# Attention on one core: the first pair's queries transposed in two copies at once, and the second pair's query load on another queue

## The chip, the cores and the metric

The kernel runs on one core of one Trainium2 chip. The metric is the device time of one execution in microseconds (us). Before the change the median of five runs is 123.73 us, the lowest 123.12 and the highest 124.13.

## The reference

Plain softmax attention over 8 batches of 8 heads, 512 positions and 64 features per head, float32 in and out:

```
scores = einsum('bhqd,bhkd->bhqk', q, k) / sqrt(64)
attn   = softmax(scores, axis=-1)
out    = einsum('bhqk,bhkd->bhqd', attn, v)
```

## The kernel before

**Tiling.** The 64 heads are taken in 32 pairs. A pair's q, k and v (256 KB each) are loaded whole, as tiles of 128 partitions by 2 heads by 4 rows by 64 features: every partition holds 4 successive rows of each head. They are cast to float16, q and k are transposed on TensorE (PE) so that the 64 features lie on partitions, and the transposes are copied out of PSUM by VectorE (DVE) (line 353 for pair 1, which is the second pair; line 355 for the later ones). A block of scores is one head's 128 keys by 512 queries (line 374). Two blocks make a group, and one exponential of ScalarE (ACT, line 379) of 128 by 1024 turns a group into float16 weights. There are 129 groups; six of them are raised on DVE instead (lines 393 to 435). The weights are multiplied with v and a column of ones (line 462), DVE divides (lines 440 and 441), and the result is stored.

**Order.** The order of PE and DVE work after the opening is written by a planner from fixed costs (class `Plan`), while the kernel is built; the order of the instructions on every engine is therefore fixed, and none of it depends on what the chip does. The exponentials run in one order on ACT. PE's score tiles are three deep.

**Loads.** Loads are issued by SyncE's queue (SP), in a fixed order: k and q, then v, pair after pair, some pairs ahead. The first loads stand in `first_loads` (lines 501 to 508): the first pair's keys in two halves on ACT's queue and its queries in two halves on SP's queue; then the second pair's keys on SP (line 507) and the second pair's queries on ACT (line 508). Eight completion counters are used in turn by all loads, so a ninth load is issued only when the first has landed, and so on.

**The opening** (`first_pair`, lines 514 to 598). The first pair is cast by three engines: DVE takes queries 0 and 1 of head 0 (line 522) and keys 0 and 1 (line 523), ACT takes queries 2 and 3 (line 524) and the whole of head 1's keys (line 526), GpSimd (POOL) takes keys 2 and 3 (line 525) and the whole of head 1's queries (line 527). The scores of the first pair need the queries on both halves of the partitions, since the keys of two chunks lie one above the other. Before, one cast copy of the queries is transposed twice, once into partitions 0 to 63 and once into partitions 64 to 127 (`t_q`, lines 545 to 547). The keys need one transpose for two chunks (`t_k`, line 541). DVE copies queries, keys, queries, keys (lines 573 to 576) and the scores follow (line 552), with the exponentials of line 559. `busy` (line 512) are matmuls on constants that keep PE running.

**The second pair.** POOL casts its keys, DVE its queries (line 331); PE transposes first the keys, then the queries (line 348); DVE copies both halves (line 353) after the last of the eight transposes; the scores of line 374 follow.

Of the kernel before, what the change touches and what calls it, by code (L numbers as in the profile page):

```python
# [9 lines left out]
FP16 = mybir.dt.float16  # L10
# [219 lines left out]
def kernel(  # L230
# [7 lines left out]
    nc = tc.nc  # L238
    B, H, S, D = q.shape
    P = 128  # L240
    NI = S // P
# [20 lines left out]
    cpool = ctx.enter_context(tc.tile_pool(name="const", bufs=1))  # L262
# [16 lines left out]
    ident = cpool.tile([P, P], FP16, name="ident")  # L279
# [13 lines left out]
    def source(src, g):  # L293
        b, h = g // ppb, 2 * (g % ppb)
        return src[b, h : h + 2].rearrange("h (p i) d -> p h i d", i=NI)

    def load_tile(g, name):
        t = lpool.tile(
            [P, 2, NI, D],
            FP32,  # L300
            tag=f"{name}32",
            name=f"{name}32_{g}",
            bufs=6,
        )
        raw.setdefault(g, {})[name] = t
        return t

    def load(g, names):
        if g >= NP:
            return  # L310
        for name in names:
            src = {"q": q, "k": k, "v": v}[name]
            t = load_tile(g, name)
            if name == "v" and g in HALVED:
                for h in range(2):
                    nc.sync.dma_start(out=t[:, h], in_=source(src, g)[:, h])
                continue
            nc.sync.dma_start(out=t[:, :, :, :], in_=source(src, g))

    def cast_v(g):  # L320
        if g >= NP:
            return
        nc.gpsimd.tensor_copy(out=vps[g % NV][:, :, :, 0:D], in_=raw[g]["v"][:, :, :, :])  # L323

    def cast_qk(g):
        if g >= NP:
            return
        t = qpool.tile([P, 2, NI, P], FP16, tag="qkp", name=f"qkp_{g}")
        for n, name in ((1, "k"), (0, "q")):
            eng = nc.vector if (g, name) == (1, "q") else nc.gpsimd  # L330
            eng.tensor_copy(  # L331
                out=t[:, n].rearrange("p i (h d) -> p h i d", h=2),
                in_=raw[g][name][:, :, :, :],
            )
        qkp[g] = t

    def feed(g):
        load(g + 5, "kqv")
        cast_qk(g + 3)
        cast_v(g + 2)  # L340
# [9 lines left out]
    def copy(g):  # L350
        if g == 1:
            for n in (1, 0):
                nc.vector.tensor_copy(out=tqk[g][:, n], in_=tps[g][:, n].rearrange("p i c -> p (i c)"))  # L353
            return
        nc.vector.tensor_copy(  # L355
            out=tqk[g][:, :, :], in_=tps.pop(g).rearrange("p n i c -> p n (i c)")
        )
# [143 lines left out]
    def first_loads():  # L501
        tk = load_tile(0, "k")
        tq = load_tile(0, "q")
        for h in range(2):
            nc.scalar.dma_start(out=tk[:, h], in_=source(k, 0)[:, h])
            nc.sync.dma_start(out=tq[:, h], in_=source(q, 0)[:, h])  # L506
        nc.sync.dma_start(out=load_tile(1, "k"), in_=source(k, 1))
        nc.scalar.dma_start(out=load_tile(1, "q"), in_=source(q, 1))

    def busy(dst, n):  # L510

        nc.tensor.matmul(dst[:, 0:n], ones[:, 0:P], ones[:, 0:n], start=True, stop=True)  # L512

    def first_pair():

        tk, tq = raw[0]["k"], raw[0]["q"]
        k16 = cpool.tile([P, 2, NI, D], FP16, name="k16_0")
        q16 = cpool.tile([P, 2, NI, D], FP16, name="q16_0")
        kt = cpool.tile([P, 2, 2, P], FP16, name="kt_0")
        qt = cpool.tile([P, 2, NI, P], FP16, name="qt_0")  # L520

        nc.vector.tensor_copy(out=q16[:, 0, 0:2], in_=tq[:, 0, 0:2])
        nc.vector.tensor_copy(out=k16[:, 0, 0:2], in_=tk[:, 0, 0:2])
        nc.scalar.copy(q16[:, 0, 2:4], tq[:, 0, 2:4])  # L524
        nc.gpsimd.tensor_copy(out=k16[:, 0, 2:4], in_=tk[:, 0, 2:4])
        nc.scalar.copy(k16[:, 1], tk[:, 1])
        nc.gpsimd.tensor_copy(out=q16[:, 1], in_=tq[:, 1])

        st0, pka, st1 = (
            ps_st.tile([P, 2, S], FP32, tag="st", name=f"st_{n}") for n in ("0a", "ka", "1")  # L530
        )
        pqa = ps_x.tile([P, 8, P], FP16, tag="x0", name="tp_qa")
        pqb = ps_x.tile([P, 8, P], FP16, tag="x1", name="tp_qb")

        pka, pkc, pqc = pka[:, 0, :], st1[:, 0, :], st1[:, 1, :]
        pka, pkc, pqc = (
            t.bitcast(FP16).rearrange("p (n c) -> p n c", c=P) for t in (pka, pkc, pqc)
        )

        def t_k(dst, h, j):  # L540
            nc.tensor.transpose(
                dst, k16[:, h, 2 * j : 2 * j + 2, :].rearrange("p i d -> p (i d)"), ident
            )

        def t_q(dst, h, i):
            for x in range(2):
                nc.tensor.transpose(dst[64 * x : 64 * x + 64], q16[:, h, i, :], ident)

        def first_scores(st, h, j, q0, q1, pt, s0, s1):
            for x in range(2):  # L550
                s = slice(64 * x, 64 * x + 64)
                nc.tensor.matmul(
                    st[:, x, s0:s1],
                    kt[s, h, j, :],
                    qt[s, h].rearrange("p i c -> p (i c)")[:, q0:q1],
                    start=True,
                    stop=True,
                )
            nc.scalar.activation(
                out=pt[:, :, q0:q1], in_=st[:, :, s0:s1], func=EXP, scale=scale  # L560
            )

        for n in range(6):
            busy(st0[:, 0], S)
        for n in range(2):
            busy(st0[:, 0], P)
        for i in range(2):
            t_q(pqa[:, i], 0, i)
        for i in range(2):
            t_q(pqc[:, i], 0, 2 + i)  # L570
        t_k(pka[:, 0], 0, 0)
        t_k(pkc[:, 0], 0, 1)
        nc.vector.tensor_copy(out=qt[:, 0, 0:2], in_=pqa[:, 0:2])
        nc.vector.tensor_copy(out=kt[:, 0, 0], in_=pka[:, 0])
        nc.vector.tensor_copy(out=qt[:, 0, 2:4], in_=pqc[:, 0:2])
        nc.vector.tensor_copy(out=kt[:, 0, 1], in_=pkc[:, 0])
        for n in range(3):
            busy(st0[:, 1], P)
        pts = [ppool.tile([P, 2, S], FP16, tag="pt", name=f"pt_{m}") for m in range(3)]
        for m in range(3):  # L580
            for x, b in enumerate(groups[m]):
                blocks[b] = pts[m][:, x, :]
        first_scores(st0, 0, 0, 0, 256, pts[0], 0, 256)
        st0b = ps_st.tile([P, 2, S], FP32, tag="st", name="st_0b")
        first_scores(st0b, 0, 0, 256, 512, pts[0], 0, 256)
        first_scores(st1, 0, 1, 0, S, pts[1], 0, S)
        for i in range(NI):
            t_q(pqb[:, i], 1, i)
        nc.vector.tensor_copy(out=qt[:, 1], in_=pqb[:, 0:4])
        pkb = ps_x.tile([P, 8, P], FP16, tag="x0", name="tp_kb")  # L590
        for j in range(2):
            t_k(pkb[:, j], 1, j)
        nc.vector.tensor_copy(out=kt[:, 1], in_=pkb[:, 0:2])
        st2 = ps_st.tile([P, 2, S], FP32, tag="st", name="st_2")
        for n in range(4):
            busy(st2[:, 0], P)
        first_scores(st2, 1, 0, 0, S, pts[2], 0, S)
        first.update(kt=kt, qt=qt)

    with tc.manual_schedule():  # L600
        first_loads()
        load(0, "v")
        for g in range(2, 5):
            load(g, "kq")
            load(g - 1, "v")
        load(4, "v")
        make_identity(nc, ident)
        for n in range(NV):
            nc.vector.memset(vps[n][:, :, :, D : D + 1], 1.0)
        first_pair()  # L610
        cast_qk(1)
        cast_v(0)
        cast_qk(2)
        cast_v(1)
        feed(0)
        do = {
            "transposes": transposes,
            "scores": scores,
            "values": values,
            "feed": feed,  # L620
            "raise": raise_,
            "copy": lambda g, b: copy(g),
            "pass": pass_,
            "norm": lambda u, n, b: normalise(u, n),
        }
        for what, *args in Plan(groups, NP, 3).run():
            do[what](*args)
# [30 lines left out]
```

## Time and profile before

| | |
|---|---|
| median of five runs | 123.73 us (123.12 to 124.13) |
| the profiled execution's own time | 124.2 us |
| its span, first to last instruction | 122.4 us |
| mean granted TensorE clock | 0.995 |
| ACT busy | 114.2 us (93% of the span) |
| PE busy | 107.7 us (88%) |
| DVE busy | 99.6 us (81%) |
| POOL busy | 74.5 us (61%) |
| DMA | 33.82 MB, 276 GB/s in the mean |

The profile is one execution, and the times of its rows are counted from the start of the span, so 1.8 us of that execution's own time lie around the span. PE is matmul, PEld is its weight load, SP and ACTq are the queues that issue loads. A busy share is the mean over stages with different limits. Matmul rows show a modelled end: what can be read from them is when one starts after another.

### The profile page before, as it was taken

The numbers are of one execution on the slowest core, as the hardware profiler recorded it, in microseconds if no ns is written. First come the engines' busy times: TensorE is split into PE (matmuls) and PEld (weight loads), VectorE is DVE, ScalarE is ACT, GpSimd is POOL, SyncE is SP. The second block draws the span as 40 slices with busy tenths as digits, with TensorE's granted clock in tenths as the row PEclk, the third lists the DMA queues.
The fourth block names the chain that finished last, engine by engine and source line by source line (L and its number), as shares of the span: only waits on it lengthen the run. The fifth ranks groups of instructions, "written<-read, shape, count | busy, mean of one in ns | idle before, by whom it ended". The sixth has DMA issues, their size and how long they took to land.

```text
span 122.4 us, 3967 instructions
## 1 busy us (share of the span) xinstructions
PE 107.7 (88%) x1565; PEld 67.2 (55%) x1565; DVE 99.6 (81%) x171; ACT 114.2 (93%) x127; POOL 74.5 (61%) x101
## 2 busy tenths in 40 slices
PE   7958788889989797998998998889999998999970
PEld 2625455546556465664655564556655655566550
DVE  1456989989989799699999999995979899976450
ACT  3697999999999999999999999999999999999960
POOL 2258889999997469497573956548783657300000
PEclk9999999999999999999999999999999999999997
DMA  3899999999979999998896999999999995213244
GB/s 117 274 334 362 378 380 383 384 365 369 363 243 274 301 326 357 334 332 273 233 267 208 310 296 298 268 334 361 313 331 320 316 273 175 73 50 126 70 141 140
DMA packets 35603, 33.82 MB, mean 276 GB/s; under 512 B 2688, under 2 KB 35584, under 8 KB 35584
## 3 DMA queue, kind: packets, MB, share of 16 engines
q1 hardware_dynamic: 34880, 32.98, 82.4%
q10 hardware_dynamic: 704, 0.59, 1.5%
q8 instruction: 12, 0.20, 0.8%
q14 instruction: 7, 0.06, 0.1%
HBM read 25.17 MB, written 8.39 MB: 274 GB/s over the span
## 4 chain that ended last, share of the span: by engine, by line
ACT 52%; PE 22%; issue 16%; DMA 5%; DVE 2%; SPq 1%; POOL 1%; ACTq 0%
ACT pt L379 52%; PE st L374 10%; PE o L462 9%; DMA k<-in_k_dram 5%; PE tp L348 3%; SPq L506 1%; DVE tqk L353 1%; PE o_last L477 1%; DVE ring L441 1%; POOL qkp L331 1%; DVE obl L490 0%; DVE rc L440 0%; DVE rc_last L489 0%; ACTq L379 0%
## 5 line engine op out<-in xcount | busy, mean ns | idle before, releaser
L379 ACT ACTIVATE pt<-st 128x1024 f16<-128x1024 f32 (+1 forms) x120 | 109.4, 1282 | 0.9 <-PE st L374 0.9
L374 PE MATMUL st<-tqk 64*128 64x512 f16 x248 | 48.1, 384 | 7.6 <-ACT pt L379 6.5
L462 PE MATMUL o<-vp,pt 128*128 128x65 f16 x1008 | 46.9, 195 | 1.6 <-ACT pt L379 1.3
L462 PEld LDWEIGHTS <-pt 128*128 128x128 f16 x1008 | 37.0, 98 | 18.7 <-issue 14.8
L331 POOL CAST qkp<-k 128x512 f16<-128x512 f32 x31 | 23.8, 767 | 25.4 <-DMA k<-in_k_dram 13.2
L323 POOL CAST vp<-v 128x512 f16<-128x512 f32 x32 | 29.4, 920 | 0.1
L374 PEld LDWEIGHTS <-tqk 64*128 64x128 f16 x248 | 13.3, 93 | 20.9 <-issue 12.8
L331 POOL CAST qkp<-q 128x512 f16<-128x512 f32 x30 | 22.9, 763 | 2.0 <-DMA q<-in_q_dram 1.1
L441 DVE TENSOR_TENSOR ring<-o,rc 128x448 f32<-128x448 f32 (+2 forms) x37 | 22.7, 612 | 1.3
L355 DVE COPY tqk<-tp 128x1024 f16<-128x1024 f16 x30 | 20.6, 686 | 3.1 <-PE tp L348 2.9
L348 PE MATMUL tp<-ident,qkp 128*128 128x128 f16 x248 | 19.6, 220 | 0.8 <-POOL qkp L331 0.8
L348 PEld LDWEIGHTS <-qkp 128*128 128x128 f16 x248 | 14.0, 98 | 7.8 <-issue 4.5
L428 DVE SCALAR_TENSOR_TENSOR y<-y,m 128x1024 f32<-128x1024 f32 x12 | 16.2, 1350 | 0.0
L440 DVE RECIPROCAL rc<-o 128x7 f32<-128x7 f32 (+2 forms) x37 | 7.4, 199 | 8.8 <-PE o L462 8.6
L393 DVE TENSOR_SCALAR z<-st 128x1024 uint32<-128x1024 f32 x6 | 7.3, 1222 | 0.9 <-PE st L374 0.9
L428 DVE SCALAR_TENSOR_TENSOR y<-m 128x1024 f32<-128x1024 f32 x6 | 8.0, 1328 | 0.0
L428 DVE SCALAR_TENSOR_TENSOR pt<-y,e 128x1024 f16<-128x1024 f32 x6 | 7.6, 1268 | 0.0
L417 DVE TENSOR_SCALAR e<-z 128x1024 uint32<-128x1024 uint32 x6 | 6.6, 1096 | 0.0
L406 DVE TENSOR_SCALAR m<-z 128x1024 uint32<-128x1024 uint32 x6 | 4.8, 805 | 0.0
L512 PE MATMUL st_0a<-const-bfloat16-1.0 128*128 128x512 bf16 (+1 forms) x11 | 3.5, 482 | 0.8 <-PEq L642 0.8
L524 ACT ACT_TABLE_LOAD x1 | 1.3, 1283 | 2.1 <-issue 2.1
L512 PEld LDWEIGHTS <-const-bfloat16-1.0 128*128 128x128 bf16 x15 | 1.7, 129 | 2.4 <-issue 2.4
(43 smaller groups left out, 17.2 us busy)
## 6 DMA issues: line engine op xcount, KB each, us to landing
out_dram<-ring SPq DMA_DIRECT2D x63, 128.0 KB, 3.7
k<-in_k_dram SPq DMA_DIRECT2D x31, 256.0 KB, 5.0
q<-in_q_dram SPq DMA_DIRECT2D x30, 256.0 KB, 5.2
v<-in_v_dram SPq DMA_DIRECT2D x27, 256.0 KB, 5.3
v<-in_v_dram SPq DMA_DIRECT2D x10, 128.0 KB, 3.9
k<-in_k_dram ACTq DMA_DIRECT2D x2, 128.0 KB, 2.9
q<-in_q_dram SPq DMA_DIRECT2D x2, 128.0 KB, 2.7
q<-in_q_dram ACTq DMA_DIRECT2D x1, 256.0 KB, 5.8
```

Of the source, the lines that this page charges most:

```text
L323: nc.gpsimd.tensor_copy(out=vps[g % NV][:, :, :, 0:D], in_=raw[g]["v"][:, :, :, :])
L331: eng.tensor_copy(out=t[:, n].rearrange("p i (h d) -> p h i d", h=2), in_=raw[g][name][:, :, :, :],)
L348: nc.tensor.transpose(tps[g][:, n, i, :], qkp[g][:, n, i, :], ident)
L355: nc.vector.tensor_copy(out=tqk[g][:, :, :], in_=tps.pop(g).rearrange("p n i c -> p n (i c)"))
L374: nc.tensor.matmul(st[:, x, :], kc, qc, start=True, stop=True)
L379: nc.scalar.activation(out=pt[:, 0:size, :], in_=st[:, 0:size, :], func=EXP, scale=scale)
L393: nc.vector.tensor_scalar(out=r["z"][:, :, :], in0=r["st"][:, :, :], scalar1=scale * 1.4426950408889634 * 2.0**23, scalar2=(127 + SHIFT) * ...
L417: nc.vector.tensor_scalar(out=r["e"][:, :, :], in0=r["z"][:, :, :], scalar1=0xFF800000, scalar2=None, op0=AluOp.bitwise_and,)
L428: nc.vector.scalar_tensor_tensor(out=r["pt"][:, :, :] if n == 3 else r["y"][:, :, :], in0=mant if n == 0 else r["y"][:, :, :], scalar=QUAR ...
L440: nc.vector.reciprocal(out=rc[:, 0:n], in_=o[:, x : x + n, D : D + 1])
L441: nc.vector.tensor_tensor(out=ring[:, u % NU : u % NU + n, :], in0=o[:, x : x + n, 0:D], in1=rc[:, 0:n].broadcast_to([P, n, D]), op=AluOp. ...
L462: nc.tensor.matmul(os[u // 7][:, u % 7, :], blocks[(g, c, h)][:, y * P : (y + 1) * P], vps[g % NV][:, h, c, :], start=(c == 0), stop=(c == ...
```

## The change

There are three edits in it. The first pair's queries are cast twice, side by side, by reading each of them two times (`broadcast_to`), so that `q16` is twice as large; each `t_q` is then one transpose of 128 by 128 which fills both halves of the partitions, in place of two of 128 by 64. In the opening's PE order the two transposes of keys stand between the first two and the last two transposes of queries. The load of the second pair's queries leaves ACT's queue and is issued by SP, directly behind the second pair's keys.

```diff
             nc.sync.dma_start(out=tq[:, h], in_=source(q, 0)[:, h])
-        nc.sync.dma_start(out=load_tile(1, "k"), in_=source(k, 1))
-        nc.scalar.dma_start(out=load_tile(1, "q"), in_=source(q, 1))
...
-        q16 = cpool.tile([P, 2, NI, D], FP16, name="q16_0")
+        q16 = cpool.tile([P, 2, NI, 2, D], FP16, name="q16_0")
...
-        nc.vector.tensor_copy(out=q16[:, 0, 0:2], in_=tq[:, 0, 0:2])
+        def twice(h, i, n):
+            return tq[:, h, i : i + n].rearrange("p i (x d) -> p i x d", x=1).broadcast_to([P, n, 2, D])
+
+        nc.vector.tensor_copy(out=q16[:, 0, 0:2], in_=twice(0, 0, 2))
         nc.vector.tensor_copy(out=k16[:, 0, 0:2], in_=tk[:, 0, 0:2])
-        nc.scalar.copy(q16[:, 0, 2:4], tq[:, 0, 2:4])
+        nc.scalar.copy(q16[:, 0, 2:4], twice(0, 2, 2))
         nc.gpsimd.tensor_copy(out=k16[:, 0, 2:4], in_=tk[:, 0, 2:4])
         nc.scalar.copy(k16[:, 1], tk[:, 1])
-        nc.gpsimd.tensor_copy(out=q16[:, 1], in_=tq[:, 1])
+        nc.gpsimd.tensor_copy(out=q16[:, 1], in_=twice(1, 0, NI))
...
         def t_q(dst, h, i):
-            for x in range(2):
-                nc.tensor.transpose(dst[64 * x : 64 * x + 64], q16[:, h, i, :], ident)
+            nc.tensor.transpose(dst, q16[:, h, i].rearrange("p x d -> p (x d)"), ident)
...
             t_q(pqa[:, i], 0, i)
+        t_k(pka[:, 0], 0, 0)
+        t_k(pkc[:, 0], 0, 1)
         for i in range(2):
             t_q(pqc[:, i], 0, 2 + i)
-        t_k(pka[:, 0], 0, 0)
-        t_k(pkc[:, 0], 0, 1)
...
         first_loads()
+        load(1, "kq")
         load(0, "v")
```

Everything behind the opening keeps its order on every engine: the planner's costs are not touched. On SP one load more stands in front of the first pair's values; on ACT one issue is gone.

## The prediction

> **What bounds the kernel now.** I read first the busy time by stage, to see which engine has no gap.
>
> ```profile
> core 0: us, PE busy (x) PEld busy (x) DVE busy (x) ACT busy (x) POOL busy (x), PEclk, DMA share, GB/s
> 10.00:34.00 24.00, 21.55 (x300) 13.15 (x298) 21.66 (x33) 24.00 (x27) 22.73 (x30) 1.00 1.07 370
> 34.00:60.00 26.00, 23.85 (x369) 15.31 (x368) 23.34 (x35) 26.00 (x29) 18.79 (x23) 1.00 0.94 297
> 60.00:90.00 30.00, 27.60 (x419) 17.71 (x418) 27.70 (x42) 30.00 (x34) 19.48 (x26) 1.00 0.93 296
> 90.00:110.00 20.00, 18.62 (x283) 11.80 (x283) 17.57 (x28) 20.00 (x23) 9.60 (x14) 1.00 0.67 216
> ```
>
> ACT is busy 100.00 of these 100 us. From 10 us on the end moves only with the moment at which ACT can start its unbroken row. ACT's timeline shows what lies before that.
>
> ```profile
> 1.65 0.46 ACTq L508 DMA_DIRECT2D q<-in_q_dram  x1
> 2.14 1.28 ACT L524 ACT_TABLE_LOAD   x1 [2.14 <-issue]
> 5.24 0.60 ACT L559 ACTIVATE pt<-st_0a 128x512 f16<-128x512 f32 x1 [0.67 <-PE st_0a L552]
> 8.02 1.05 ACT L379 ACTIVATE pt<-st 128x1024 f16<-128x1024 f32 x1
> 9.98 2.85 ACT L379 ACTIVATE pt<-st 128x1024 f16<-128x1024 f32 x3 [0.90 <-PE st L374]
> ```
>
> The first pair's exponentials run from 5.24 to 9.07 without a gap; then ACT waits 0.90 us for the second pair's scores. The chain of work that ended last starts there too, and not at the first pair:
>
> ```profile
> 1.64 5.66 DMA k<-in_k_dram
> 7.36 0.62 POOL qkp L331
> 8.03 0.69 PE tp L348 x8
> 8.74 0.77 DVE tqk L353 x2
> 9.55 0.41 PE st L374 x2
> 9.98 23.95 ACT pt L379 x26
> ```
>
> DVE's timeline shows the second branch, which is as late: the queries' cast, 7.48 to 8.25, ahead of the last four transposes.
>
> ```profile
> 7.48 0.77 DVE L331 CAST qkp<-q 128x512 f16<-128x512 f32 x1 [0.93 <-DMA q<-in_q_dram]
> ```
>
> The last stretches concern the loads: the transfer rate falls to half just when the second pair is due.
>
> ```profile
> 2.50:3.50 1.00, 1.00 (x5) 0.38 (x3) 0.14 (x1) 0.99 (x2) 0.00 (x0) 1.00 1.09 374
> 3.50:4.50 1.00, 1.00 (x13) 0.69 (x12) 0.55 (x3) 0.56 (x2) 0.74 (x2) 1.00 0.66 174
> 4.50:6.00 1.50, 1.50 (x23) 0.92 (x21) 0.63 (x4) 0.83 (x3) 0.00 (x0) 1.00 0.91 306
> 6.00:7.50 1.50, 0.94 (x10) 0.27 (x7) 0.57 (x3) 1.50 (x3) 0.14 (x1) 1.00 0.95 291
> 7.50:10.00 2.50, 1.41 (x16) 0.87 (x16) 1.50 (x3) 1.60 (x3) 2.34 (x4) 1.00 1.07 378
> ```
>
> So the change has two halves of unlike weight. What it does to the first pair can only lengthen or shorten a wait of 0.90 us; what it does to the landing of the second pair reaches the end.
>
> **First pair, casts.** Every query cast writes twice as much. On ACT the rows are 0.30 us for 128x128 and 0.40 for 128x256, so +0.10, at 3.43. POOL's goes from 0.40 (128x256) to 0.61 (its 128x512 rows): 4.03 to 4.64, still ahead of its transposes at 5.47. DVE's has 0.23 for 128x128; the next rows are 0.77 for a 128x512 cast beside a POOL cast, and 0.682 as the shortest 128x1024 operation between SBUF tiles (line 406). Another 128 columns are thus +0.18 by the one and +0.07 by the other; I take +0.10, since no POOL work lies beside it at 3.37. The reading of an element twice is in no row; at its worst it costs the upper value.
>
> **First pair, transposes.** Line 547's 16 become 8. That sounds like a halving, but the eight of head 0 take four steps of 0.107 us, 3.65 to 3.97: four start within 0.21 us (3.65, then 3.86), in pairs. Head 1's eight start at 5.47 and its keys at 5.82. The full transposes that follow start 0.08 to 0.11 us apart. Four full ones cost what eight half ones did, so PE's gain from the count is nothing. What can be gained is the gap behind them: the last pair starts at 3.97 and the keys' transpose at 4.21, 0.24 us instead of 0.11. Here the Trainium skill speaks on both sides (TensorEngine Tiling, Key Properties): tiles of the array work independently, so that two half-width transposes may run side by side, which speaks against a gain from this change, and a switch of the tiling mode drains the engine, which speaks for one. By the first alone the edit would be worth 0.00, by the second the 0.13 us that the rows show.
>
> New order: queries 3.75, 3.86, keys 3.96, 4.07, queries 4.18, 4.28. DVE's first copy starts at 4.22 instead of 4.11; but its second, the keys', which waited until 4.54, now follows at once at about 4.45. The scores start at 4.77 instead of 4.86 and the first exponential at 5.15 instead of 5.24: 0.1 us earlier, between 0.1 later and 0.2 earlier with the bounds of the casts. Behind the exponentials of the pair this moves 9.07 to 8.97. ACT's wait grows from 0.9 to 1.0 us, and the end does not move. If that cover were gone, it would be a gain of 0.1.
>
> **The load that is moved.** On ACT 0.46 us of issue go at 1.65, so the table load ends at 2.96 instead of 3.42. The cast behind it still waits for the queries that DVE sees at 3.37: 0.06 us, off the path. On SP the issue of 0.46 us stands in front of the values at 2.11 and the third pair's keys at 2.63, which go to 2.57 and 3.09. The third pair's queries were issued at 3.52 because of a counter (the ninth load), so the delay ends there at 0.1 us or less. The load that waited until 7.48 now waits for the second pair's keys and not its queries. With eight loads of 256 KB in flight this costs nothing.
>
> **When the second pair lands.** The keys landed at 7.30 (1.64 + 5.66) and the queries at 7.46 (ended DVE's wait at 7.48). On one queue the keys no longer share with the queries, and should land earlier; the queries come behind them. Bounds for the queries: early, if the stretch 3.5 to 7.5 went at the 375 GB/s of the stretches around it, its 174 + 459 + 437 = 1070 KB would take 2.85 us and the landing would be 6.3. Late, if the keys still landed at 7.30 and the queries one load behind: successive loads end 0.61 to 0.74 us apart (SP is released at 9.43, 10.04, 10.72 and 11.46), so 8.04; or 8.2, from an issue at 2.11 and 6.1 us, the longest that a 256 KB load of the first 10 us took to land. Between them I take 7.4: the bytes ahead of the queries are the same, the keys' 256 KB, and only the values no longer run beside their tail.
>
> **What follows from the landing.** DVE's cast took 0.77 us since POOL's cast of the keys (7.36 to 7.98) lay beside it. With the keys earlier, POOL is done, and its next cast waits for values that land later. A lone cast: 0.23 plus three times 0.07 = 0.43, the row without POOL; at worst 0.77 again. From the cast's end to the exponential everything stays as it is, 9.98 − 8.25 = 1.73: DVE's first copy waits for all eight transposes, so early keys alone gain nothing. The new start is 7.40 + 0.02 + 0.43 + 1.73 = 9.58, which is 0.40 us earlier, 7.46 − 7.40 + 0.34. With the bounds: 6.3 gives 8.48, but ACT is not free before 8.97, so at most 1.0 us gained; 8.2 and 0.77 give 10.72, 0.74 lost. Would others hold back an ACT that runs 0.4 us earlier? POOL is the fullest, 22.73 of 24.00 us. Its fourth pair's queries are cast by 12.12 and used by the transposes that begin at 12.52, and the fifth's by 14.62 for 15.04: 0.4 us is just covered, and the transposes run about a pair ahead of the scores.
>
> Sum: the profiled execution's 124.2 − 0.4 = 123.8, 0.47 us above the median of the runs in both cases; from the median, 123.73 − 0.40 = 123.3 us.
>
> **Rivals.** *The slow start goes.* If the dip to 174 GB/s comes from two queues sharing the engines, one queue removes it. For: 7.50 to 10.00, where SP's queue is alone, has 378 GB/s. Against: 2.50 to 3.50 had both queues and 374 GB/s. The second pair lands by 6.7, ACT's wait closes, and the time is 123.73 − 1.0 = 122.7.
>
> *The queries queue up.* The one feed on SP serves the keys first, and the queries start only then. For: loads one behind another end 0.61 to 0.74 us apart. Against: the engines were not full then. From a landing at 7.80 (9.98 − 1.73 − 0.43 − 0.02) on it decides for slower; at 8.2 with a contended cast it is 0.74 later, 124.5.
>
> *It doesn't do what it says.* The transposes save no array time, and the landing stays with a cast as long as before: 123.7.
>
> On the skill's DMA: Bandwidth & Descriptors (Issuing engines are not separate DMA queues), loads from all engines run on the same 16 engines and a second issuer saves only issue time. By it the queries land as before; no row here compares the two.
>
> **How the numbers follow.** My forecast, 0.2 to 0.7 us gained, 0.45, its own range 123.0 to 123.5; the slow start 0.27; the queue 0.16; no effect 0.12. About 0.5%, 0.62 us, is what a measurement of this kernel can tell from no change. Faster by more: the slow start, and 0.11 of my forecast, 0.38. Slower by more: queries that land from 8.1 on with a contended cast, 0.11 of the queue's 0.16. The rest, 0.51, is within. The range goes from 122.6, below the slow start's 122.7, to 124.1, inside the queue's case.
>
> **What would show it.** Right: the keys' POOL cast starts before 6.9, the queries' DVE cast near 7.4 in about 0.43 us, the first exponential at 5.1 to 5.2, ACT's wait behind 9 us near 0.6. Wrong: an ACT wait above 0.9, or a first exponential after 5.5; a wait of ACT past 10 us would show that the loads or POOL hold it back.

## Result and the profile after

The changed kernel takes 123.16 us in the median of 44 runs (122.75 to 123.88), the kernel before 123.60 us in the median of 79. The ratio is 0.9966, 95% interval 0.9956 to 0.9976: 0.34% or 0.42 us faster. The forecast was 123.3 us, 0.40 us gained. Its profiled execution took 123.32 us, with a span of 121.5 us. Every ratio below is taken against the kernel before, run beside the kernel in question. Executions more than 1.5% longer than the fastest of their kernel, at a lower granted clock, stay out of the ratios and of the table below: at most three in any other set of runs, but four of twelve with the loads by head and seven of twelve with the queries two loads behind, and whether those two edits bring them about is open.

ACT's timeline after, as in the prediction (start, length in us, line, what; the last column is idle time and who ended it):

```profile
1.65 1.28 ACT L526 ACT_TABLE_LOAD   x1 [1.65 <-PEq L644]
4.76 0.60 ACT L560 ACTIVATE pt<-st_0a 128x512 f16<-128x512 f32 x1 [0.40 <-PE st_0a L553]
7.55 1.04 ACT L379 ACTIVATE pt<-st 128x1024 f16<-128x1024 f32 x1
9.26 3.77 ACT L379 ACTIVATE pt<-st 128x1024 f16<-128x1024 f32 x4 [0.66 <-PE st L374]
```

The unbroken row of exponentials begins at 9.26 us, 0.72 us earlier than before, and ACT still waits 0.66 us for it. Not all of the 0.72 us belongs to the change: the first query cast starts at 3.11 us here and at 3.37 before, and it starts at 3.18 and 3.40 in two profiles of one kernel (the queue alone, below). Behind it ACT is as full as before (busy time by stage after):

```profile
10.00:34.00 24.00, 21.49 (x301) 13.05 (x299) 22.58 (x34) 24.00 (x28) 22.25 (x29) 1.00 1.06 365
34.00:60.00 26.00, 23.89 (x368) 15.39 (x365) 22.97 (x34) 26.00 (x30) 19.21 (x24) 1.00 0.95 308
60.00:90.00 30.00, 27.42 (x414) 17.37 (x412) 26.98 (x44) 30.00 (x34) 19.88 (x25) 1.00 0.93 294
90.00:110.00 20.00, 18.80 (x288) 12.00 (x288) 17.57 (x27) 20.00 (x24) 9.24 (x13) 1.00 0.68 216
```

POOL's and DVE's timelines after, the second pair's casts:

```profile
6.45 0.61 POOL L331 CAST qkp<-k 128x512 f16<-128x512 f32 x1 [2.04 <-DMA k<-in_k_dram]
7.10 0.43 DVE L331 CAST qkp<-q 128x512 f16<-128x512 f32 x1 [0.96 <-DMA q<-in_q_dram]
```

The keys are cast 0.91 us earlier than before, the queries 0.38 us earlier, and the queries' cast takes 0.43 us instead of 0.77. The chain that ended last shows what I had not foreseen. It begins with another load:

```profile
2.61 5.20 DMA v<-in_v_dram
7.87 0.63 POOL vp L323
8.54 0.29 PE o L462 x4
8.83 0.41 PE st L374 x2
9.26 2.85 ACT pt L379 x3
```

In PE's fixed order four matmuls on the first pair's values stand ahead of the second pair's scores. Their cast ends at 8.50 and they are through at 8.83; DVE's second copy ends at 8.02 + 0.76 = 8.78. The two branches are level.

The stretches in which the load rate dipped, after:

```profile
3.50:4.50 1.00, 0.89 (x13) 0.71 (x12) 0.59 (x5) 0.42 (x2) 0.80 (x2) 1.00 0.65 206
4.50:6.00 1.50, 1.32 (x16) 0.80 (x16) 0.69 (x4) 1.24 (x3) 0.00 (x0) 1.00 0.98 323
6.00:7.50 1.50, 0.99 (x8) 0.34 (x8) 0.54 (x2) 1.50 (x2) 0.61 (x1) 1.00 1.00 339
```

The dip is still there, 206 GB/s instead of 174; over the four microseconds 1199 KB moved instead of 1070. One profile is not enough to read the dip by. In the seven profiles of this document with this order of loads the stretch from 3.5 to 4.5 us has 95 to 300 GB/s, in the two with the load on ACT 174 and 106. The bytes of the four microseconds do part the two orders: 1142 to 1284 KB against 1070 and 1018.

**One number that sums up a run.** ACT's work from the start of its sixth exponential (the second pair's first) to the end of its last takes 108.33 to 108.37 us in the first ten rows of this table, so the time of an execution can be read from that start. All times in us; "fifth ends" is when the first pair's last exponential is through.

| profiled execution | fifth ends | sixth starts | own time | own time − sixth |
|---|---|---|---|---|
| before | 9.08 | 9.98 | 124.20 | 114.2 |
| after | 8.60 | 9.26 | 123.32 | 114.1 |
| after, again | 9.28 | 9.73 | 123.76 | 114.0 |
| queue alone | 9.02 | 9.08 | 123.15 | 114.1 |
| queue alone, again | 9.31 | 9.38 | 123.43 | 114.1 |
| transposes alone, again | 9.19 | 9.91 | 124.01 | 114.1 |
| queries behind the values | 9.33 | 9.41 | 123.46 | 114.0 |
| POOL beside | 8.88 | 9.84 | 123.93 | 114.1 |
| early copy | 8.96 | 9.37 | 123.40 | 114.0 |
| queries two loads behind | 8.63 | 9.95 | 124.00 | 114.1 |
| by head and early copy | 8.87 | 9.21 | 123.99 | 114.8 |
| split copy | 9.26 | 9.15 | 123.37 | 114.2 |

The two profiles of the changed kernel differ by 0.44 us, as much as the whole change is worth; so a cause is read from the rows of a profile and a worth from the ratio.

### The profile page after: what moved, and what is told of

Its sections match the earlier page's. It is cut to its first block, busy times and chain, and to the rows that moved or that the text cites. A ratio compares the mean times of both kernels' runs of the same rounds, so it can differ in the third digit from the quotient of the medians.

```text
span 121.5 us, 3951 instructions
## 1 busy us (share of the span) xinstructions
PE 107.1 (88%) x1557; PEld 67.0 (55%) x1557; DVE 98.4 (81%) x171; ACT 114.3 (94%) x127; POOL 74.9 (62%) x101
## 4 chain that ended last, share of the span: by engine, by line
ACT 54%; issue 19%; PE 17%; DMA 4%; SPq 1%; DVE 1%; POOL 1%; ACTq 0%
ACT pt L379 54%; PE st L374 7%; PE o L462 7%; DMA v<-in_v_dram 4%; PE tp L348 2%; SPq L318 1%; SPq L506 1%; PE o_last L477 1%; DVE ring L441 1%; POOL vp L323 1%; DVE obl L490 0%; DVE rc L440 0%; DVE rc_last L489 0%; ACTq L379 0%
## 5 line engine op out<-in xcount | busy, mean ns | idle before, releaser
L331 POOL CAST qkp<-k 128x512 f16<-128x512 f32 x31 | 25.2, 812 | 22.8 <-DMA k<-in_k_dram 12.3
L331 POOL CAST qkp<-q 128x512 f16<-128x512 f32 x30 | 25.7, 856 | 2.4 <-DMA q<-in_q_dram 2.2
L323 POOL CAST vp<-v 128x512 f16<-128x512 f32 x32 | 25.4, 794 | 0.9 <-DMA v<-in_v_dram 0.8
L417 DVE TENSOR_SCALAR e<-z 128x1024 uint32<-128x1024 uint32 x6 | 6.1, 1022 | 0.0
```

What stands on the lines that cost most here:

```text
L331: eng.tensor_copy(out=t[:, n].rearrange("p i (h d) -> p h i d", h=2), in_=raw[g][name][:, :, :, :],)
L417: nc.vector.tensor_scalar(out=r["e"][:, :, :], in0=r["z"][:, :, :], scalar1=0xFF800000, scalar2=None, op0=AluOp.bitwise_and,)
```

## The experiments

My theory: the end follows the second pair's landing and the queries' cast, so the moved load carries the gain and the first pair's transposes carry nothing to the end. Rivals: the transposes bring it; the slow start of the loads was due to two queues.

### Each half alone

Queue alone (kernel before, `e1`, and once more as `e11`):

```diff
-        nc.scalar.dma_start(out=load_tile(1, "q"), in_=source(q, 1))
+        nc.sync.dma_start(out=load_tile(1, "q"), in_=source(q, 1))
```

> The kernel before with the load of the second pair's queries moved to SP behind its keys; the first pair as before. If the end hangs on that landing and on a cast without POOL beside it, this has the whole gain of the change: 0.3 to 0.5 us under the kernel before, DVE's cast of the second pair's queries 0.43 us, ACT's first exponential about 1.9 us after the first landing as before. If the gain came from the first pair's transposes, it is within 0.1 us of the kernel before.

Measured: ratio to the kernel before 0.9993 (0.9970 to 1.0016), median 123.43 against 123.66 us. DVE's cast took 0.43 us, as expected, and was through at 7.26 us. ACT waited only 0.06 us behind the first pair. The chain that ended last starts with no load here; it runs through PE's work on the first pair:

```profile
6.64 0.39 PE st L552 x2
7.03 0.22 PE st L374 x2
7.25 0.57 PE tp L348 x8
7.84 0.77 DVE tqk L353 x2
8.65 0.41 PE st L374 x2
```

In PE's fixed order the second pair's transposes stand behind the first pair's last scores, and PE came to them at 7.25 us. The second pair's scores were there at 9.06 us, the first pair's exponentials ended at 9.02. Two bounds are level here. My sum had the second of them, at 8.97; the first, PE's order, was missing from it.

Transposes alone (changed kernel, `e2`, and once more as `e12`):

```diff
-        load(1, "kq")
+        load(1, "k")
+        nc.scalar.dma_start(out=load_tile(1, "q"), in_=source(q, 1))
```

> The changed kernel with the load of the second pair's queries issued from ACT again, as before. If the end hangs on the second pair, this is within 0.15 us of the kernel before, though the first exponential starts 0.1 to 0.2 us earlier counted from the first query cast, and ACT's wait after the first pair is longer for it (about 1.0 us). If the transposes bring the gain, it is 0.3 us or more under the kernel before.

Measured: 1.0011 (0.9982 to 1.0040), 123.62 us. No gain is seen.

The intervals of this pair did not part the two, so I ran both again on another chip.

> The queue move alone once more (the same kernel as the first experiment), beside the transposes alone on one chip. Two bounds stand now: the end of the first pair's exponentials, which the profiles put between 8.5 and 9.4 us depending on when the granted clock becomes full, and the second pair's chain. If the queue move carries the gain and the first pair's form is worth nothing, it is 0.3 to 0.5 us under the kernel before; if both halves are needed, 0.1 to 0.25.

Measured: 0.9965 (0.9940 to 0.9990), 123.38 against 123.70 us: as much as the whole change. ACT's wait was 0.06 us again, and the chain the same: PE came to the second pair's transposes at 7.55 us, though the queries' cast was through at 7.22.

> The transposes alone once more. If the second pair's chain, which is as before here, sets the end in nearly every execution, it is within 0.1 us of the kernel before. If the first pair often sets it, 0.1 to 0.25 us under it. DVE's cast of the second pair's queries should lie beside POOL's cast of the keys again, 0.75 to 0.8 us.

Measured: 0.9993 (0.9969 to 1.0017). DVE's cast lay beside POOL's again and took 0.64 us, less than the 0.75 expected, and ACT's wait was 0.72 us (timelines of the transposes alone):

```profile
7.54 0.64 DVE L331 CAST qkp<-q 128x512 f16<-128x512 f32 x1 [0.77 <-DMA q<-in_q_dram]
9.91 2.85 ACT L379 ACTIVATE pt<-st 128x1024 f16<-128x1024 f32 x3 [0.72 <-PE st L374]
```

The transposes alone show no gain in either run. The queue move has 0.07% and 0.35% in its two, against 0.34% and 0.37% of both halves; by the medians it is 0.19% and 0.26% against 0.36% twice. Whether the transposes add something to it, 0.1 to 0.2 us where the first pair is the bound, these runs do not part.

### The cast beside POOL

`e4`, the changed kernel with one POOL cast more behind the keys' cast:

```diff
         cast_qk(1)
+        spare = cpool.tile([P, 2, NI, D], FP16, name="spare")
+        nc.gpsimd.tensor_copy(out=spare[:, :, :, :], in_=raw[1]["k"][:, :, :, :])
         cast_v(0)
```

> The changed kernel with one more POOL cast of 128x512 (the second pair's keys into a tile that nobody reads) behind the cast of the second pair's keys, so that POOL is busy while DVE casts the queries. If a POOL cast beside it is what made that DVE cast 0.77 us instead of 0.43, it is about 0.7 us again and the time is 0.25 to 0.35 us over the changed kernel. If the two engines do not disturb each other, the cast stays at 0.43 us and the time stays within 0.1 us of the changed kernel.

Measured: 1.0003 (0.9981 to 1.0025) against the kernel before, so 0.37% above the changed kernel's 0.9966: by the ratio the gain is gone, 0.46 us where 0.25 to 0.35 were expected. The medians, 123.44 against 123.66 us, leave about half of it, so the ratio shows the direction and not the size. POOL's and DVE's timelines of this kernel:

```profile
7.22 0.62 POOL L615 CAST spare<-k 128x512 f16<-128x512 f32 x1
7.32 0.80 DVE L331 CAST qkp<-q 128x512 f16<-128x512 f32 x1 [0.96 <-DMA q<-in_q_dram]
```

0.80 us beside POOL, 0.43 without. The sixth exponential starts 9.84 − (7.32 + 0.80) = 1.72 us after the cast's end, as the prediction's 1.73. So in this execution the longer cast costs its 0.37 us one for one.

The rows also show where such a cast ends. In the three profiles where a POOL cast lies beside it, DVE's cast ends 0.28 us after POOL's: 8.25 after 7.97 in the kernel before, 8.18 after 7.90 with the transposes alone, 8.12 after 7.84 here. It does so whether it started 0.13, 0.25 or 0.10 us after POOL's, which is why it took 0.64 us and not 0.75 in the second of them.

### The landing

`e3`, the changed kernel with the queries behind the first pair's values:

```diff
-        load(1, "kq")
-        load(0, "v")
+        load(1, "k")
+        load(0, "v")
+        load(1, "q")
```

> The changed kernel with the second pair's queries issued on SP behind the first pair's values. They land one load of 256 KB later, 0.6 to 0.75 us. If the landing sets the end one for one, it is 0.6 to 0.75 us over the changed kernel, 0.2 to 0.35 over the kernel before; more by 0.3 if POOL's cast of the values then lies beside DVE's cast. If the landing has slack, it equals the changed kernel.

Measured: 0.9980 (0.9956 to 1.0005), 0.14% or 0.17 us above the changed kernel's ratio, and not 0.6: a miss. The queries' cast started at 7.26 us, inside the 7.10 to 7.58 that the changed kernel's two profiles show. One place in the queue is less than the scatter of a landing. Nor could this profile show it at the end: its chain runs through PE's work on the first pair, as with the queue alone, and PE came to the second pair's transposes at 7.57 us.

`e10`, with the queries behind the third pair's keys too:

```diff
-        load(1, "kq")
-        load(0, "v")
-        for g in range(2, 5):
-            load(g, "kq")
+        load(1, "k")
+        load(0, "v")
+        for g in range(2, 5):
+            load(g, "k")
+            if g == 2:
+                load(1, "q")
+            load(g, "q")
```

> The changed kernel with the second pair's queries issued on SP behind the first pair's values and the third pair's keys, two loads of 256 KB later. They land about 1.3 us later than in the changed kernel, so the second pair's chain is the bound in every execution. If the end follows that landing one for one, it is 1.0 to 1.4 us over the changed kernel, and the start of ACT's sixth exponential plus 108.33 us is the end of its last; if something else fills the gap, less.

Measured: 1.0042 (1.0007 to 1.0076), from five executions, 0.76% or 0.94 us above the changed kernel's ratio. ACT's timeline:

```profile
7.59 1.04 ACT L379 ACTIVATE pt<-st 128x1024 f16<-128x1024 f32 x1
9.95 2.85 ACT L379 ACTIVATE pt<-st 128x1024 f16<-128x1024 f32 x3 [1.31 <-PE st L374]
```

The queries' cast came at 7.79 and ACT waited 1.31 us. In this profile the end follows the landing, 1.73 us from the cast's end to the sixth exponential again, but the landing itself moved by less than two loads: 0.2 to 0.7 us against the changed kernel's two, not 1.3. The 0.94 us of the ratio are more than this landing explains; what the rest is stays open.

### What is late next

`a2` is the changed kernel once more, beside the three that follow.

> The changed kernel itself, beside the next three on one chip. From the profiles so far ACT's work from its sixth exponential to its last takes 108.33 to 108.37 us in every undisturbed one, so the time should differ between runs by the start of that sixth exponential alone: about 114.1 us plus that start. Expected 0.3 to 0.5 us under the kernel before.

Measured: 0.9963 (0.9936 to 0.9991). The chain that ended last starts with the queries this time, and not with the values:

```profile
2.11 5.44 DMA q<-in_q_dram
7.58 0.44 DVE qkp L331
8.06 0.41 PE tp L348 x4
8.50 0.77 DVE tqk L353 x2
9.30 0.41 PE st L374 x2
```

`e5`, the keys' copy right behind their transposes:

```diff
             nc.tensor.transpose(tps[g][:, n, i, :], qkp[g][:, n, i, :], ident)
+        if g == 1 and n == 1:
+            nc.vector.tensor_copy(out=tqk[g][:, n], in_=tps[g][:, n].rearrange("p i c -> p (i c)"))
...
-            for n in (1, 0):
+            for n in (0,):
```

> The changed kernel with the copy of the second pair's transposed keys right behind their four transposes, ahead of the queries' transposes, so that DVE need not wait for all eight. Of the two copies, 0.76 us, about 0.35 then lie ahead of the queries' transposes. If the second pair's chain sets the end, ACT's sixth exponential starts up to 0.36 us earlier, as far as ACT is free by then: 0.2 to 0.36 us under the changed kernel. If ACT is free no earlier (first pair sets the end), no difference.

Measured: 0.9992 (0.9967 to 1.0016), no faster. PE's timeline shows why:

```profile
8.04 0.38 PE L348 MATMUL tp<-ident,qkp 128*128 128x128 f16 x4 [0.52 <-DVE tqk L350]
```

The queries' transposes write the PSUM tile that DVE reads the keys from, and in this kernel they wait for that copy. The wait that was taken away came back 0.52 us long: from the cast's end at 6.98 to the sixth exponential it took 2.39 us instead of 1.73. Only about half of the 0.66 us more is that wait. The keys' transposes could start no earlier than 7.20, when PE was through with the first pair's scores; with the order of the changed kernel and the lengths of the queue-alone chain above, the sixth exponential would have started at about 9.02 (an estimate: 7.20 + 9.07 − 7.25) instead of 9.37.

`e6`, the second pair's loads by head, and `e7`, that and the early copy:

```diff
-        load(1, "kq")
+        for name, src in (("k", k), ("q", q)):
+            t = load_tile(1, name)
+            for h in range(2):
+                nc.sync.dma_start(out=t[:, h], in_=source(src, 1)[:, h])
```

> The changed kernel with the second pair's keys and queries loaded head by head on SP, four loads of 128 KB. Loads of one head landed on all 16 engines within 0.35 us of each other, loads of two heads within 1.9 us. If that spread belongs to the form of the load, the queries land earlier by up to 0.7 us and ACT's wait closes: 0.2 to 0.6 us under the changed kernel. If the spread comes from the time and the queue, nothing changes; the two more issues of 0.4 us may cost the loads behind them.

Measured: 1.0017 (0.9990 to 1.0044), slower than the changed kernel's 0.9963 on the same chip. No profile of it is compared here.

> The early copy and the loads by head together. If the second pair's chain sets the end, ACT has no wait behind the first pair and the first pair becomes the bound: sixth exponential at the end of the fifth, 0.4 to 0.66 us under the changed kernel. If one of the two edits does nothing, no better than the better one alone.

Measured: 1.0008 (0.9986 to 1.0030). The queries' cast started at 6.32 us, but the third pair's queries, issued at 4.51 instead of 3.64, became the next wait (chain that ended last):

```profile
4.51 5.18 DMA q<-in_q_dram
9.75 0.62 POOL qkp L331
```

ACT waited 0.33 us behind the first pair and 0.25 us again at 11.1. Two further issues stand ahead of the third pair's loads, and the gain is given back one pair later.

`e9`, smaller copies in another order, and the first values behind the second pair's first scores:

```diff
-            for n in (1, 0):
-                nc.vector.tensor_copy(out=tqk[g][:, n], in_=tps[g][:, n].rearrange("p i c -> p (i c)"))
+            for n, i0, i1 in ((0, 0, NI), (1, 0, 1), (1, 1, NI)):
+                nc.vector.tensor_copy(
+                    out=tqk[g][:, n, i0 * P : i1 * P],
+                    in_=tps[g][:, n, i0:i1].rearrange("p i c -> p (i c)"),
+                )
...
-        for what, *args in Plan(groups, NP, 3).run():
+        steps = Plan(groups, NP, 3).run()
+        n = next(n for n, s in enumerate(steps) if s[0] == "values")
+        n1 = next(n for n, s in enumerate(steps) if s[0] == "scores" and s[1] == 4)
+        steps.insert(n1, steps.pop(n))
+        for what, *args in steps:
```

> The changed kernel with the second pair's copies in another order and size (queries first, then the first 128 keys, then the other 384) and with the first unit of values behind the second pair's first scores instead of ahead of them, so that these scores wait neither for the rest of the keys nor for the cast of the values. From the cast's end to ACT's sixth exponential 1.73 us become about 1.5. Where the second pair's chain is the bound that is 0.2 us; where ACT is still at the first pair, nothing: 0.05 to 0.2 us under the changed kernel, 0.4 to 0.65 under the kernel before.

Measured: 0.9962 (0.9942 to 0.9982), level with the changed kernel (0.9966 and 0.9963). ACT has no wait left in its profile:

```profile
7.32 1.02 ACT L563 ACTIVATE pt<-st 128x1024 f16<-128x1024 f32 x1 [0.28 <-PE st L556]
8.24 4.75 ACT L382 ACTIVATE pt<-st 128x1024 f16<-128x1024 f32 x5
```

In that execution the first pair sets the end, and nothing on the second pair's side can show; the 0.05 to 0.2 us expected under the changed kernel did not come. No version tried here is measurably faster than the changed kernel.

## Why the prediction was right, and where not

**ACT from 10 us on.** Right: 24, 26, 30 and 20 us of the same stretches again, and 108.33 to 108.37 us from the sixth exponential to the last one's end. POOL, with 22.25 of 24.00 us, held nothing back.

**The load that is moved.** Right in sign and worth; its terms were off in opposite ways. The lone cast, 0.43 us forecast, is 0.42 to 0.43 us in every profile with no POOL cast beside it (0.34 us gained), and a POOL cast beside it made it 0.80 us again. The landing of the queries I moved by 0.06 us, from 7.46 to 7.40. In the seven profiles with the changed order of loads (after, again, the two with the queue alone, POOL beside, early copy, split copy) the queries' cast starts at 7.10, 7.58, 6.83, 6.80, 7.32, 6.55 and 6.87, mean 7.01, against 7.48 and 7.54 with the load on ACT. So the mis-sized term is the landing: about 0.5 us, or 0.38 when counted from the first pair's first cast, where I had 0.06. The scatter is as large as the term. Behind it stand the keys, for which the prediction gave no number: in these seven they land at 5.41 to 6.89 us, before at 7.30, and the queries follow them by 0.65 to 0.71 us (1.40 once) instead of by 0.16.

**Why the sum still held.** Cast and landing together would be 0.7 to 0.8 us. Three things that I had taken as fixed or as free cut it. I had put the end of the first pair's exponentials at 8.97; it lay between 8.60 and 9.33. I had taken 1.73 us from the cast's end to the exponential as fixed; that holds where the transposes wait for the casts, but with the queue alone it took 1.81 and 2.16 us, because PE still had the first pair's scores ahead of the transposes. And I wrote that 0.46 us of issue in front of the values costs nothing; they are level with the queries in the profile after, since PE's order puts them ahead of the scores. The forecast of 0.40 us is near the measured 0.42 partly because these errors cancel, which is luck.

**The transposes.** Full transposes start 0.107 us apart (3.50, 3.61, 3.71 in PE's rows after), just as pairs of half ones did, and the gap of 0.24 us ahead of the keys is gone. The Trainium skill names a drain when the tiling mode changes (TensorEngine Tiling, Key Properties). The lost 0.13 us agree with it, but no run here separates that drain from another cause. The first exponential starts 1.82 us after the first query cast in the mean of nine profiles of the new form and 1.92 in the mean of three of the old, the 0.1 us forecast; single profiles scatter by 0.3 to 0.4 us. At the end of the fifth exponential nothing of it is left: 5.82 us after the first query cast in both means. Compared where PE's matmuls quicken at nearly the same time, that distance is 5.62 us in the old form and 5.59 in the new (queue alone, POOL beside), and 6.13 against 5.92 in a late pair (the two repeats). On their own the transposes show no gain at the end, as forecast: 1.0011 and 0.9993. What they add beside the moved load is open.

**The rivals.** The slow start did not go: the dip is 206 GB/s in the profile after and 95 to 300 with one queue in all, as said above. What was right in that rival is the earlier landing. The other rival was half right. The queries do queue up behind the keys, 0.65 us or more after them, as its late bound had it; but that bound left the keys at 7.30 us, and they landed 0.4 to 1.9 us earlier. So the queries did not land as before either. Why the keys of a lone queue land so much earlier, no run here shows.

## What to carry to other kernels

When one engine runs without a gap, look for the last moment at which that row can still start, and list every chain that must be through by then, each with its own scatter: the second latest bounds what any edit can gain. A load's place in the queue acts on its own landing and on which engines work side by side when it lands; here the second was the better known part. Taking a wait away in a fixed order shows at once who stands next in line: another load, the copy of a shared PSUM tile, or the work of the pair before on the same engine.

## What the hardware showed that I had not expected

PE's matmuls of 128 columns start 0.107 us apart at first and about 0.056 us apart later. The moment at which they quicken differs from execution to execution though the program and its first matmuls do not. In PE's timeline of the changed kernel the transposes of the keys take 0.27 and 0.22 us, since the quicker rate begins there (the next two starts follow 0.057 and 0.055 us apart):

```profile
3.71 0.27 PE L543 MATMUL st_ka<-ident,k 128*128 128x128 f16 x1
3.82 0.22 PE L543 MATMUL st<-ident,k 128*128 128x128 f16 x1
```

and of the same kernel run again 0.31 each, at the slower rate until about 6.2 us:

```profile
3.73 0.31 PE L543 MATMUL st_ka<-ident,k 128*128 128x128 f16 x1
3.83 0.31 PE L543 MATMUL st<-ident,k 128*128 128x128 f16 x1
```

Between these two the first pair's fifth exponential ends 5.48 and 6.09 us after the first query cast. That is a scatter of 0.6 us in one of the two bounds of this kernel, more than the change is worth. The granted clock of these stretches is given as 1.00 in both, so it has to be read from the rows.
